# Steps of the mixers beneath the GEMMs, emitted with a priority 24 instructions later

## The chip, the cores and the metric

The kernel runs on one core of one Trainium2 chip, as one program. The metric is the device time of a launch in microseconds; the median of several runs is compared. A profiled execution gives the trace that is read here. Its engines are PE (TensorE), DVE (VectorE), ACT (ScalarE), POOL (GpSimd) and SP (SyncE, which issues most DMAs).

## The reference

One inference step of a decoder trunk with two layers and D = 1024, for a prompt of 1024 tokens and for 8 samples of 8 new tokens each, in float32. Cut to what matters:

```
for layer in range(2):
    h = rmsnorm(x, norm_pre_mix[layer])
    if layer == 0: # half of the heads GLA (linear attention with gates), half a 31-tap causal conv
        z = h @ w_in_even
        oa = rmsnorm(gla_scan(q, k, v, log_a, state)) * silu(r)
        c = silu(layernorm(causal_dwconv(ga * sigmoid(gg), conv_buf)))
        y = concatenate([oa, c]) @ w_out_even
    else:          # three groups of dilated attention with a T5 bias, and a chunked gMLP
        z = h @ w_in_odd
        oc = softmax-weighted sum of dilated_attn(q, kv, window, dilation, bias) over 3 groups
        od = gelu(du) * (tril(sgu_w) @ layernorm(gelu(dv)) + sgu_b)
        y = concatenate([oc, od]) @ w_out_odd
    x = x + rmsnorm(y, norm_post_mix[layer])
    h = rmsnorm(x, norm_pre_ffn[layer])
    up = causal_dwconv(h @ w_up, ffn_buf)      # 3 taps, 2 * 2816 channels
    g, val = split(up)
    x = x + rmsnorm((gelu(g) * val) @ w_down, norm_post_ffn[layer])
```

The outputs are y of both groups and the new states and K/V buffers.

## The kernel before

**Two halves.** The tokens are two halves. A holds 512 tokens of the prompt and is one piece of 512 columns; B holds the other 512 and the 64 sample tokens, as two pieces of 288 columns. Activations lie as [channels, tokens]. While PE does the large products of one half, the small work of the other half (its mixer, its norms) is done beneath them.

**GEMM products.** `gemm` multiplies a chunk of weights, [up to 1024, 128], with the activations in three passes, so that products of rounded parts give float32 exactness: high part of the weight by the activation's `hi` and by its `lo`, low part of the weight by `hi`. The PSUM tiles of a GEMM are named `g`, those of all other work `m`; so `g<-hi,whi`, `g<-lo,whi` and `g<-hi,wlo` are GEMM products and `m<-...` are products or transposes of mixers and norms, both mostly at line 227 (`mm`) and 224 (`tr`). A chunk is loaded by a DMA of SP into `raw`; `whi` is rounded from it on POOL (line 206) or ACT, and `wlo` = raw - whi is made by DVE or POOL (line 371). `fill` issues these three under `high_priority(self.ahead)`, ahead = 400 from the second projection on.

**ConvFFN.** `ffn_up` does a pair of GEMMs, copies the result to `u`, does the three taps on ACT and DVE (the tiles `c`, line 200), and makes `c * c` on DVE (line 197) and of it `hi` on ACT (line 209) and `lo` on DVE. `ffn` goes through six parts of 4 or 3 such pairs; the pairs of a part stand between the down products of the part before, which need them.

**Background.** `during` installs a generator `self.bg`, whose steps emit a few instructions each and then yield their weight; after each k of a GEMM `gemm` calls `pump`, which takes as many steps as the pace asks for; `drain` takes what is left at once.

```
    def pump(self, units):
        if self.bg is None:
            return
        self.acc += units * self.rate
        while self.acc > 0:
            w = next(self.bg, None)
```

What stands beneath what, with the times of the profiled execution before:

- up to about 380 us: the projection of layer 0, `in_even`, of A with the load of B's x, then with A's conv and GLA, then of B; `out_proj` of A, and the rest of `in_even` of B with A's norms.
- 412 to 870: the first FFN, of A in layer 0, above `mix0`: B's conv (tiles `cv`, 240 rows on DVE at line 200), B's GLA (`gla`, line 959 copies queries into `w`; `gla_sample` multiplies `w` and `km`), copies of cache rows and the FFN's state (`fst`).
- 870 to 935: the end of that FFN, the norms between it and layer 1 (`ss` holds sums of squares, which a product with `ones` adds up; line 427 is `sq_add`'s on POOL), and B's `out_proj`.
- then `in_odd` of A, with B's norms; 1100 to 1440 lies in the FFN of B in layer 0, above `mix1(A)` (A's attention and gMLP).
- 1740 to 1850: `in_odd` of B, above B's `gmlp` and `sample_scores`. gMLP's normalised values use a tile with the tag `kt`; PE multiplies it with the weights `sg`.
- then the FFN of A in layer 1 above `mix1(B)`, and last, with 2420 to 2756 in it, the FFN of B.

**What sets the order.** The program is scheduled ahead of time. Each instruction has a priority, its place in the order in which the code emits it; for each engine the scheduler goes through a simulated time line of its own and puts next, among the instructions whose inputs it thinks ready, the one with the earliest priority. On the chip each engine then works through its list strictly in that order. `tc.high_priority(n)` moves what is emitted within it n places forward.

Of the kernel before, what the change touches and what calls it, by code (L numbers as in the profile page):

```python
# [15 lines left out]
PSUM = bass.MemoryType.PSUM  # L16
# [33 lines left out]
def t5_bucket(dist):  # L50
    """Bucket of a distance, from the shapes alone."""
    max_exact = N_BUCKETS // 2
    dist = np.asarray(dist)
    d32 = np.maximum(dist, 1).astype(np.float32)
    ratio = np.log(d32 / np.float32(max_exact)).astype(np.float32) / np.float32(math.log(MAX_DIST / max_exact))
    large = max_exact + (ratio * np.float32(N_BUCKETS - max_exact)).astype(np.int32)
    large = np.minimum(large, N_BUCKETS - 1)
    return np.where(dist < max_exact, dist, large)


def shape_constants():
    """Masks, selections and one-hot tables that depend on the shapes only."""
# [4 lines left out]
    m = []  # L67
# [9 lines left out]
    # query order inside a dilation class: partition (j, i) of class r is position 16 i + 4 j + r  # L77
# [13 lines left out]
    # rows (batch, part, head, query) of a pair of dilation classes -> columns (batch, head, query) of a class and head pair  # L91
# [5 lines left out]
    # columns (batch, head, query) -> (batch, class pair, head, class, query)  # L97
# [12 lines left out]
    # new keys of a sample batch: rows (head, query), columns new keys; steps 0 and 1 of dilation 4, step 0 of 16  # L110
# [10 lines left out]
# projections of the second half before and after the out projection of the first  # L121
VB1, VB2 = ("u", "glr", "q", "k", "v0"), ("v1", "r")
# paces of the work that runs between products, cache tiles loaded ahead
VQ, LQ, SA, QS, QM, VW, SV = 12, 6, 4, 14, 90, 0.4, 3
# (half, layer): down product of the last part but one before which the last pair of up projections runs
# [13 lines left out]
class Kern:  # L139
    def __init__(self, ctx, tc, I, O):  # L140
# [19 lines left out]
        # of 16 weight chunks: rounded on ACT instead of Pool, remainder on Pool instead of DVE  # L160
        self.nw, self.hi_act, self.lo_pool = 0, 0, 0

# [11 lines left out]
    def wk(self, i, shape, dt=F32):  # L174
        """Working tile of at most 2 KB per partition, slot i."""
# [38 lines left out]
    def copy(self, out, in_):  # L214
        """Copies that either engine can take, in turn unless DVE is loaded."""
# [13 lines left out]
    def rstd(self, out, in_, scale):  # L229
        """out = (in * scale + eps) ** -0.5 for a few columns."""  # L230
# [5 lines left out]
    def during(self, gen, weight, products, wait=0):  # L236
        """Spread gen, whose steps yield their weights, over that many products of [1024, 128] with 512 columns,
        from the one after the first wait."""
# [3 lines left out]
    def pump(self, units):  # L242
# [3 lines left out]
        while self.acc > 0:  # L246
            w = next(self.bg, None)
# [12 lines left out]
    def merge(*gens):  # L260
        """Steps of several (generator, weight), each at the pace of its weight."""
# [20 lines left out]
    def vec_consts(self):  # L282
        nc, I, cp = self.nc, self.I, self.cp
        # per-channel vectors: rows of 128 channels, turned into columns
# [19 lines left out]
    def mix_consts(self):  # L304
# [14 lines left out]
        # conv taps of the Conformer module: [channel, tile, tap]  # L319
# [7 lines left out]
        # twice, for the high and the low part of its input  # L327
# [3 lines left out]
        # ConvFFN taps: [channel, (w0 | w1 | w2 | b), tile]  # L331
# [42 lines left out]
    def gemm(self, h, hs, w, k0, c0, m):  # L374
        """PSUM tiles (one per piece) of w[k0.., c0:c0+m]^T @ h."""
# [11 lines left out]
    def gemm_narrow(self, h, hs, w, c0, m):  # L387
        """Like gemm for few columns, in two passes: rows m.. of the result are the low part of the weights."""
# [13 lines left out]
    def split(self, h, src, tag_pool=None):  # L402
        """Exact two-part form of an activation tile."""
# [11 lines left out]
    def sq_add(self, h, ss, src, k):  # L415
        """Add the squares of a tile to the partial sums ss; when it is urgent, DVE sums every other tile."""
# [12 lines left out]
    def rms(self, h, src):  # L429
        """Reciprocal rms of each token from the sums of squares in the columns of src."""  # L430
# [6 lines left out]
    def rb(self, h, ss, r=None):  # L437
        """[128, n] tile whose rows all hold the reciprocal rms of each token."""
# [23 lines left out]
    def pre_norm(self, h, xt, ss, name, l, r=None):  # L462
        """RMSNorm of the tiles in xt (consumed); returns the split operand tiles."""
# [73 lines left out]
    def finish(self, h, y, ss, xs):  # L537
        """Last residual norm and the output rows, in steps; 14 in all."""
# [33 lines left out]
    def ffn_state(self, l):  # L572
        """Sample rows of the ConvFFN buffer as [channel, tile, (batch, row)]."""
# [12 lines left out]
    def ffn_up(self, h, hs, l, j):  # L586
        """One pair of up-projected tiles through conv, gelu and product; returns the split activation."""
# [36 lines left out]
    def x_rows(self, h, tmp, xs, out):  # L624
        """Token-major rows of a residual kept as channel tiles, as [block][half of the channels]; tiles in the arena of tmp."""
# [18 lines left out]
    def last_down(self, h, tmp, acts, l, part, y, xt):  # L644
        """Last down products, residual norm and output rows of the samples' half, for one range of tokens after the other:
        the norm of a range runs under the products of the next."""
# [9 lines left out]
        def rows(blocks, c1, sq):  # L656
            """r times the weighted sums, plus the residual."""
# [1341 lines left out]
```

## Time and profile before

| | |
|---|---|
| three runs | 2784.78, 2800.16, 2804.39 us (median 2800.16) |
| the profiled execution, from first to last instruction | 2798.1 us |
| PE busy | 2673.0 us, 96% |
| PE weight loads | 2366.4 us, 85% |
| DVE busy | 1757.6 us, 63% |
| ACT busy | 973.7 us, 35% |
| POOL busy | 1035.2 us, 37% |
| mean granted TensorE clock | 0.967 |
| moved by DMA | 355.83 MB, mean 127 GB/s |

The profiled execution has no time of its own beside its span; the span is what stands for it here. A busy PE is one on which a product is under way; the clock is the share of full speed that was granted to it. In rows of the trace the first number is the start in us, the second the duration, then come engine, line, operation, what it writes and from what (partitions x elements), how many; in brackets stands how long the engine had been idle before and what released it.

### The profile page before, as it was taken

To read this page: it belongs to the slowest core of one execution; us is meant where nothing else is said; L and a number is where in the kernel's file an instruction comes from. 1 tells how busy PE (TensorE), PEld (TensorE's weight loads), DVE (VectorE), ACT (ScalarE), POOL (GpSimd) and SP (SyncE) were. 2 spreads that over 40 slices of the span, in tenths; PEclk is the share of its full clock that TensorE was granted. 3 is DMA by queue.
4 is the path that set the end of the run, shared out by engine and by line. 5 is a ranking of instruction groups with operands and counts; after the bars stand their busy time and mean duration, and the time that the engine had idled before them with its cause. 6 is when DMAs were issued, how large, how long until landed. Compare 5 with 4: busy or idle time off the path is not lost.

```text
span 2798.1 us, 44057 instructions
## 1 busy us (share of the span) xinstructions
PE 2673.0 (96%) x16517; PEld 2366.4 (85%) x16517; DVE 1757.6 (63%) x3057; ACT 973.7 (35%) x2036; POOL 1035.2 (37%) x1159
## 2 busy tenths in 40 slices
PE   7989999999999999999999999889999898999999
PEld 6779887787888879999999979878877687999998
DVE  4888359899577655555547783556654348655555
ACT  4343445433453222324223241123332343322223
POOL 2322333432326434332437543552112165433333
PEclk9999989999999999999999999999989898999999
DMA  6433354445444554232224436884444143422232
GB/s 211 120 102 90 88 184 151 146 159 163 156 139 125 182 165 139 76 94 68 85 68 134 126 107 191 238 233 130 135 127 122 37 144 106 129 78 79 85 91 83
DMA packets 505005, 355.83 MB, mean 127 GB/s; under 512 B 29547, under 2 KB 461282, under 8 KB 504015
## 3 DMA queue, kind: packets, MB, share of 16 engines
q1 hardware_dynamic: 504791, 353.01, 41.6%
q8 instruction: 131, 2.15, 0.3%
q14 instruction: 83, 0.68, 0.1%
HBM read 306.43 MB, written 75.97 MB: 137 GB/s over the span
## 4 chain that ended last, share of the span: by engine, by line
PE 64%; DVE 10%; DMA 5%; POOL 4%; issue 3%; ACT 2%; SPq 1%; POOLq 0%; DVEq 0%; ACTq 0%
PE g L227 55%; PE m L227 7%; DVE cv L200 3%; PE m L224 2%; DMA kc<-qr 1%; DVE wlo L371 1%; DVE c L200 1%; POOL whi L206 1%; SPq L188 1%; DVE y L197 1%; DVE y L200 1%; POOL w L1677 1%; DVE lo L197 1%; POOL ss L427 1%; DMA raw<-in_w_up 1%
## 5 line engine op out<-in xcount | busy, mean ns | idle before, releaser
L227 PE MATMUL g<-hi,whi 128*128 128x288 f32 (+2 forms) x4440 | 1279.3, 336 | 32.2 <-ACT hi L209 9.7
L227 PE MATMUL g<-lo,whi 128*128 128x288 f32 (+2 forms) x4440 | 1268.1, 334 | 5.1 <-DVE lo L197 5.0
L227 PE MATMUL g<-hi,wlo 128*128 128x288 f32 (+1 forms) x4416 | 1260.9, 334 | 2.8 <-DVE wlo L371 2.6
L227 PEld LDWEIGHTS g<-hi,whi 128*128 128x128 f32 (+1 forms) x4440 | 777.5, 192 | 107.5 <-issue 25.5
L227 PEld LDWEIGHTS g<-lo,whi 128*128 128x128 f32 (+1 forms) x4440 | 776.8, 191 | 71.2 <-DVE lo L197 7.2
L227 PEld LDWEIGHTS g<-hi,wlo 128*128 128x128 f32 x4416 | 773.5, 192 | 70.5 <-issue 7.8
L371 DVE TENSOR_TENSOR wlo<-raw,whi 128x1024 fp32r<-128x1024 f32 (+2 forms) x382 | 404.5, 1059 | 443.4 <-POOL whi L206 347.6
L206 POOL TENSOR_SCALAR whi<-raw 128x1024 fp32r<-128x1024 f32 (+2 forms) x307 | 318.4, 1037 | 762.8 <-PE g L227 659.3
L371 POOL TENSOR_TENSOR wlo<-raw,whi 128x1024 fp32r<-128x1024 f32 (+2 forms) x94 | 193.0, 2055 | 418.1 <-ACT whi L209 349.7
L200 DVE SCALAR_TENSOR_TENSOR c<-u,dw,c 128x512 f32<-128x512 f32 (+3 forms) x528 | 316.6, 637 | 43.7 <-ACT c L212 42.2
L209 ACT ACTIVATE whi<-raw 128x1024 fp32r<-128x1024 f32 (+3 forms) x171 | 145.0, 848 | 361.7 <-PE g L227 219.3
L209 ACT ACTIVATE u<-g 128x224 f32<-128x224 f32 (+2 forms) x352 | 129.1, 398 | 249.7 <-PE g L227 236.9
L200 DVE SCALAR_TENSOR_TENSOR cv<-u,cvw,cv 128x512 f32<-128x512 f32 (+21 forms) x240 | 202.2, 853 | 4.0 <-ACT cv L212 2.1
L197 DVE TENSOR_TENSOR y<-y,g 128x288 f32<-128x288 f32 (+3 forms) x240 | 120.4, 525 | 117.4 <-PE g L227 117.0
L212 ACT ACTIVATE c<-g,dw 128x288 f32<-128x288 f32 (+1 forms) x264 | 173.1, 657 | 2.3 <-DMA out_s_ffn_conv<-rw 1.3
L209 ACT ACTIVATE hi<-c 128x512 fp32r<-128x512 f32 (+1 forms) x88 | 57.9, 658 | 222.6 <-DVE c L197 222.5
L427 POOL TENSOR_TENSOR ss<-ss,sq 128x512 f32<-128x512 f32 (+1 forms) x75 | 119.9, 1599 | 41.1 <-ACT sq L212 40.6
L212 ACT ACTIVATE c<-c 128x512 f32<-128x512 f32 (+1 forms) x88 | 57.9, 658 | 138.4 <-DVE c L200 131.9
L212 ACT ACTIVATE sq<-y 128x512 f32<-128x512 f32 (+3 forms) x103 | 63.3, 622 | 85.5 <-POOL ss L427 41.9
L200 DVE SCALAR_TENSOR_TENSOR y<-y,vec,rb 128x512 f32<-128x512 f32 (+1 forms) x104 | 87.5, 908 | 7.2 <-ACT rb L209 7.2
L1677 POOL TENSOR_TENSOR w<-kc,kc 128x512 f32<-128x512 f32 x48 | 65.1, 1368 | 69.4 <-DMA kc<-qr 57.8
L600 POOL COPY last<-u 128x2 f32<-128x2 f32 x88 | 45.8, 521 | 121.6 <-ACT u L209 102.3
(288 smaller groups left out, 2350.6 us busy)
## 6 DMA issues: line engine op xcount, KB each, us to landing
raw<-in_w_up SPq DMA_DIRECT2D x176, 512.0 KB
raw<-in_w_down SPq DMA_DIRECT2D x128, 256.0 KB
raw<-in_w_in_odd SPq DMA_DIRECT2D x44, 512.0 KB
raw<-in_w_in_even SPq DMA_DIRECT2D x40, 512.0 KB
out_s_kv<-in_cache_c_w SPq DMA_DIRECT2D x32, 512.0 KB
raw<-in_w_down SPq DMA_DIRECT2D x64, 192.0 KB
xl<-x SPq DMA_DIRECT2D x40, 256.0 KB
kc<-in_cache_c_w SPq DMA_DIRECT2D x80, 128.0 KB
```

The costliest lines, as they stand in the source:

```text
L188: self.nc.sync.dma_start(out, in_)
L197: self.nc.vector.tensor_tensor(out=out, in0=a, in1=b, op=op)
L200: self.nc.vector.scalar_tensor_tensor(out=out, in0=a, scalar=s, in1=b, op0=op0, op1=op1)
L206: self.nc.gpsimd.tensor_scalar(out=out, in0=a, scalar1=s1, scalar2=s2, op0=op0, op1=op1)
L209: self.nc.scalar.activation(out, in_, AF.Copy, scale=scale)
L212: self.nc.scalar.activation(out, in_, func, **kw)
L224: self.nc.tensor.transpose(out, in_, self.ident[:k, :k])
L227: self.nc.tensor.matmul(out, l, r, start=start, stop=stop)
L371: eng.tensor_tensor(out=wlo[:, :nk, :m], in0=raw[:, :nk, :m], in1=whi[:, :nk, :m].bitcast(F32), op=ALU.subtract)
L427: eng.tensor_tensor(out=t, in0=t, in1=sq, op=ALU.add)
L600: self.nc.gpsimd.tensor_copy(self.last2[l][:, jt, :], u[:, 512:514])
L1677: nc.gpsimd.tensor_tensor(out=pr, in0=kc.rearrange("p i c -> p (i c)"), in1=q.rearrange("p i c -> p (i c)"), op=ALU.mult)
```

## The change

`pump` takes its steps with a priority 24 places later. `high_priority(-24)` adds 24 to the place of each instruction that a step emits, DMAs included, so that it competes with GEMM instructions (products, weight fills, evictions, conv taps) that are emitted up to 24 instructions behind it. Fills within keep their own 400 places. `drain` takes its steps as before, and so does code that runs norms in a plain loop. Nothing else changes but comments, which shifts lines by 2 or 3 (197 is 199 after the change, 200 is 202, 209 is 211, 224 is 226, 227 is 229).

```diff
         self.ahead = 0
+        self.lag = 24
...
         while self.acc > 0:
-            w = next(self.bg, None)
+            with self.tc.high_priority(-self.lag):
+                w = next(self.bg, None)
             if w is None:
```

Every engine has the same instructions as before; what differs is their order. Three places, each first as it is before and then as it is now.

The first is on DVE in the first FFN (near 640 us of the trace). `c_1133` and `c_1143` are tiles of the FFN's conv, `cv_1110` and `cv_1228` those of B's conv in `mix0`, and line 197's row is the product `c * c` of which `hi` is made.

```order
L200 SCALAR_TENSOR_TENSOR c_1133_5623<-u_1134_5624,dw0_828,c_1133_5623 128x510
L200 SCALAR_TENSOR_TENSOR cv_1110_5441<-us_811_3799,cvw_823,cv_1110_5441 128x64
L200 SCALAR_TENSOR_TENSOR c_1143_5696<-u_1144_5697,dw0_828,c_1143_5696 128x511
L200 SCALAR_TENSOR_TENSOR cv_1228_6213<-u_530_2276,cvw_823,cv_1228_6213 128x512
L200 SCALAR_TENSOR_TENSOR cv_1228_6213<-us_812_3800,cvw_823,cv_1228_6213 128x64
L200 SCALAR_TENSOR_TENSOR cv_1110_5441<-u_494_2033,cvw_823,cv_1110_5441 128x512
L197 TENSOR_TENSOR c_1127_5584<-c_1127_5584,c_1133_5623 128x512
L200 SCALAR_TENSOR_TENSOR cv_1110_5441<-us_811_3799,cvw_823,cv_1110_5441 128x64
L200 SCALAR_TENSOR_TENSOR c_1143_5696<-u_1144_5697,dw0_828,c_1143_5696 128x510
```

```order
L202 SCALAR_TENSOR_TENSOR cv_1228_6213<-u_530_2276,cvw_823,cv_1228_6213 128x512
L202 SCALAR_TENSOR_TENSOR c_1143_5696<-u_1144_5697,dw0_828,c_1143_5696 128x511
L202 SCALAR_TENSOR_TENSOR c_1133_5623<-u_1134_5624,dw0_828,c_1133_5623 128x510
L202 SCALAR_TENSOR_TENSOR cv_1228_6213<-us_812_3800,cvw_823,cv_1228_6213 128x64
L202 SCALAR_TENSOR_TENSOR cv_1110_5441<-u_494_2033,cvw_823,cv_1110_5441 128x512
L202 SCALAR_TENSOR_TENSOR cv_1110_5441<-us_811_3799,cvw_823,cv_1110_5441 128x64
L202 SCALAR_TENSOR_TENSOR cv_1228_6213<-u_530_2276,cvw_823,cv_1228_6213 128x512
L202 SCALAR_TENSOR_TENSOR c_1143_5696<-u_1144_5697,dw0_828,c_1143_5696 128x510
L199 TENSOR_TENSOR c_1127_5584<-c_1127_5584,c_1133_5623 128x512
L202 SCALAR_TENSOR_TENSOR cv_1228_6213<-us_812_3800,cvw_823,cv_1228_6213 128x64
L202 SCALAR_TENSOR_TENSOR cv_1110_5441<-u_494_2033,cvw_823,cv_1110_5441 128x512
```

The product stands at DVE's place 832 before and 824 now: rows of `cv`, emitted earlier and given the later priority, now stand behind it.

The second is on PE at the end of the first FFN (870 us). `g_1531`, `g_1536` and `g_1541` are the last down products of A; `m_1479` and `m_1481` belong to `gla_sample`, `m_1496` and `m_1502` to the FFN's state.

```order
L227 MATMUL g_1531_7780<-hi_1403_7195,wlo_1530_7776 128x512
L227 MATMUL m_1479_7546<-w5_1442_7377,km_1478_7544 64x128 x8
L227 MATMUL m_1481_7560<-w5_1442_7377,km_1480_7558 64x128 x8
L224 MATMUL m_1496_7638<-ident_87,w3_1491_7605 128x64 x4
L224 MATMUL m_1502_7663<-ident_87,w1_1501_7661 128x16 x4
L227 MATMUL g_1531_7780<-hi_1452_7419,whi_1529_7775 128x512
L227 MATMUL g_1531_7780<-lo_1453_7420,whi_1529_7775 128x512
L227 MATMUL g_1531_7780<-hi_1452_7419,wlo_1530_7776 128x512
L227 MATMUL g_1536_7800<-hi_1369_7026,whi_1534_7795 128x512
```

```order
L229 MATMUL g_1541_7820<-hi_1452_7419,wlo_1540_7816 128x512
L229 MATMUL m_1464_7469<-ident_87,zt_1473_7506 64x128
L229 MATMUL m_1465_7470<-ident_87,zt_1473_7506 64x128
L229 MATMUL m_1464_7469<-w5_1442_7377,AT_935_4410 64x128
L229 MATMUL m_1464_7469<-ident_87,zt_1473_7506 64x128
L229 MATMUL m_1465_7470<-w5_1442_7377,AT_936_4412 64x128
L229 MATMUL m_1465_7470<-ident_87,zt_1473_7506 64x128
L229 MATMUL m_1475_7518<-w5_1442_7377,km_1474_7516 64x128 x8
L229 MATMUL m_1477_7532<-w5_1442_7377,km_1476_7530 64x128 x8
L229 MATMUL m_1479_7546<-w5_1442_7377,km_1478_7544 64x128 x8
L229 MATMUL m_1481_7560<-w5_1442_7377,km_1480_7558 64x128 x8
L226 MATMUL m_1496_7638<-ident_87,w3_1491_7605 128x64 x4
```

Before, these mixer rows stand between the down products, with `g_1531`, `g_1536` and `g_1541` still to come; now all of them, and the product of `ones` with `ss_1507` too, stand behind the last of `g_1541` and ahead of `g_1610`, the first product of B's `out_proj`.

The third is on PE in `in_odd` of B (1740 us and on). `m_3174` is a product of gMLP with the tile `kt`; `g_3164` and `g_3165` are the two pieces of one GEMM, `g_3190` and `g_3191` those of the next.

```order
L227 MATMUL g_3164_17258<-hi_2934_16034,whi_3162_17253 128x288
L227 MATMUL g_3165_17259<-hi_2934_16034,whi_3162_17253 128x288
L227 MATMUL g_3164_17258<-lo_2935_16035,whi_3162_17253 128x288
L227 MATMUL m_3174_17317<-sg_3067_16843,kt_3148_17201 64x128 x4
L227 MATMUL g_3165_17259<-lo_2935_16035,whi_3162_17253 128x288
L227 MATMUL g_3164_17258<-hi_2934_16034,wlo_3163_17254 128x288
L227 MATMUL g_3165_17259<-hi_2934_16034,wlo_3163_17254 128x288
L227 MATMUL g_3164_17258<-hi_2936_16051,whi_3162_17253 128x288
```

```order
L229 MATMUL g_3164_17258<-hi_2936_16051,wlo_3163_17254 128x288
L229 MATMUL g_3165_17259<-hi_2936_16051,wlo_3163_17254 128x288
L229 MATMUL g_3190_17371<-hi_2902_15893,whi_3188_17366 128x288
L229 MATMUL g_3191_17372<-hi_2902_15893,whi_3188_17366 128x288
L229 MATMUL g_3190_17371<-lo_2903_15894,whi_3188_17366 128x288
L229 MATMUL g_3191_17372<-lo_2903_15894,whi_3188_17366 128x288
L229 MATMUL g_3190_17371<-hi_2902_15893,wlo_3189_17367 128x288
L229 MATMUL g_3191_17372<-hi_2902_15893,wlo_3189_17367 128x288
L229 MATMUL m_3174_17317<-sg_3067_16843,kt_3148_17201 64x128 x4
L229 MATMUL g_3190_17371<-hi_2904_15910,whi_3188_17366 128x288
```

`m_3174` stood within the first GEMM; now the rest of that GEMM and six products of the next stand ahead of it.

## The prediction

> **What bounds the kernel now.** I read the page first, from its busy shares to its slices and its chain of waits.
>
> ```profile
> span 2798.1 us, 44057 instructions
> PE 2673.0 (96%) x16517; PEld 2366.4 (85%) x16517; DVE 1757.6 (63%) x3057; ACT 973.7 (35%) x2036; POOL 1035.2 (37%) x1159
> PE 64%; DVE 10%; DMA 5%; POOL 4%; issue 3%; ACT 2%; SPq 1%; POOLq 0%; DVEq 0%; ACTq 0%
> ```
>
> TensorE is busy in 2673.0 of 2798.1 us, so an order of instructions alone can win at most the 125.1 us in which it stands idle, and what its clock loses after such stops. The chain agrees: 64% PE. What matters is thus where PE stops, and whether the order changes there. I cut the run into its stages, and asked for PE's waits in the three where the new order moves mixer products against GEMM products and PE stops at all.
>
> ```profile
> core 0: us, PE busy (x) PEld busy (x) DVE busy (x) ACT busy (x) POOL busy (x), PEclk, DMA share, GB/s
> 412.00:560.00 148.00, 138.11 (x639) 111.55 (x639) 135.04 (x242) 73.07 (x115) 54.71 (x36) 0.94 0.45 146
> 560.00:660.00 100.00, 93.93 (x519) 75.57 (x518) 99.81 (x185) 38.58 (x64) 28.67 (x23) 0.97 0.44 142
> ...
> 870.00:935.00 65.00, 58.44 (x385) 55.15 (x384) 47.36 (x55) 21.16 (x42) 35.19 (x20) 0.92 0.42 135
> 1100.00:1440.00 340.00, 339.88 (x2384) 313.25 (x2383) 185.10 (x424) 111.69 (x294) 116.03 (x213) 1.00 0.29 84
> 1740.00:1850.00 110.00, 100.11 (x731) 96.87 (x731) 58.82 (x95) 21.46 (x54) 57.11 (x48) 0.95 0.86 245
> 2420.00:2756.00 336.00, 336.00 (x2525) 335.99 (x2525) 178.05 (x308) 92.03 (x230) 119.93 (x209) 1.00 0.28 82
> ...
> PE m L227 <- POOL w L959: 6.8, 1, 6.8
> PE g L227 <- ACT hi L209: 6.0, 2, 5.1
> PE g L227 <- DVE lo L197: 2.4, 2, 2.0
> PE m L227 <- DVE k L197: 0.7, 1, 0.7
> ...
> PE m L227 <- POOL ss L427: 3.4, 1, 3.4
> PE m L227 <- DVE ss L427: 1.6, 1, 1.6
> PE g L227 <- DVE lo L197: 1.6, 1, 1.6
> ...
> PE m L227 <- DVE kt L197: 8.3, 4, 3.2
> ```
>
> From 1100 to 1440 and from 2420 to 2756 us PE idles 0.12 and 0.00 us: there, with mix1(A) or no mixer, nothing can be won, although mix1(A)'s products move by about 20 GEMM products. The first FFN (412 to 870) loses 15.9 us in four kinds of wait, its end (870 to 935) 6.6, the layer-1 projection of the samples' half (1740 to 1850) 8.3 to the mixer's kt tile. That is 30.8 us of idle PE, all of it at places that move. DVE is full in the first FFN: 99.81 of 100 us between 560 and 660. Waits elsewhere, as those at the other handovers, stand at the same place in both orders, and I count them as unchanged.
>
> **The change part by part.** Nothing is added or removed; every number below is a move. Two prices first.
>
> ```profile
> 535.82 0.39 PE L227 MATMUL g<-hi,whi 128*128 128x512 f32 x1
> 542.39 0.39 PE L227 MATMUL g<-hi,wlo 128*128 128x512 f32 x1
> ...
> 1768.71 0.43 PE L227 MATMUL g<-hi,whi 128*128 128x288 f32 x2
> 1768.97 0.42 PE L227 MATMUL g<-lo,whi 128*128 128x288 f32 x2
> ```
>
> The first two rows are the first and the last of 30 GEMM products of the first half, so one costs 6.57 / 29 = 0.227 us; two of the samples' half cost 0.26, one 0.13. Now the stops.
>
> ```profile
> 550.31 1.65 PE L227 MATMUL m<-w,k 128*128 128x128 f32 x6 [6.77 <-POOL w L959]
> 551.61 0.77 PE L227 MATMUL g<-hi,whi 128*128 128x512 f32 x1
> ...
> 554.32 0.53 PE L227 MATMUL g<-hi,whi 128*128 128x512 f32 x1
> ...
> 536.56 1.26 POOL L959 COPY w<-q 64x256 f32<-64x256 f32 x1 [2.83 <-DVE q L197]
> 538.76 11.50 POOL L959 COPY w<-q 64x256 f32<-64x256 f32 x1 [0.94 <-DVE q L197]
> 550.22 2.35 POOL L371 TENSOR_TENSOR wlo<-raw,whi 128x1024 fp32r<-128x1024 f32 x1
> 552.53 1.75 POOL L600 COPY last<-u 128x2 f32<-128x2 f32 x2
> ...
> 643.31 1.22 PE L227 MATMUL g<-hi,whi 128*128 128x512 f32 x2 [5.06 <-ACT hi L209]
> ...
> 638.87 0.74 DVE L200 SCALAR_TENSOR_TENSOR c<-u,dw,c 128x510 f32<-128x510 f32 x1
> 641.91 0.69 DVE L197 TENSOR_TENSOR c<-c,c 128x512 f32<-128x512 f32 x1
> ```
>
> *The stop at 643.31.* It waits for hi, which ACT makes from the c-by-c product at 641.91, which DVE reaches late because it works through the conv's cv rows without a pause. In the new order that product stands 8 DVE places earlier (the first place shown above). From 638.87 to 641.91 six rows take 3.0 us, half a microsecond each, so 8 places are 4 us. PE comes there about as late as before. I take -4.
>
> *The stop at 550.31.* PE waits for a copy that held POOL 11.50 us. In the new order this mixer product stands 24 GEMM products later, 24 x 0.227 = 5.4 us of cover, but on POOL the copy now stands behind the 2.35 us weight remainder and one of the two small copies (1.75 for two), so it may come 3.2 us later. 5.4 - 3.2 = 2.2; I take -2, between -6.8 (gone) and +3 (the remainder's own input late).
>
> The Trainium skill, "SBUF — State Buffer", section "SBUF: two separate sides", says that VectorE and GpSimd share one port pair as an exclusive lock, the loser standing still for the whole instruction. This speaks against the change here: DVE's work is the same, so the 11.50 us stay. By it this term cannot pass -2.2; the trace agrees in so far as the copy at 536.56, of the same shape, took 1.26 us.
>
> *The other waits of the first FFN* (0.9 + 2.4 + 0.7 us): PE's places don't change at the first two, DVE's GEMM rows come some five places earlier. I take -1.5, between 0 and -4.
>
> *The clock.* The rows from 551.61 to 554.32 are the seven products behind that stop: six steps in 2.71 us, 0.45 each instead of 0.227, so 1.35 us lost. After a stop that shrinks under 2 us I count this as won: -1.5 for the stop at 643.31, none for 550.31.
>
> The Trainium skill, "TensorE: Matmul & The Clock Gate", Part 1, has the clock halve after an idle window of about 3.4 us and return after as much work. By that rule up to 1.7 us hang on each longer stop, and nothing on shorter ones; the spacing of 0.45 after the stop of 6.77 us agrees, and the sum would not differ by more than 1 us.
>
> *The end of the first FFN.*
>
> ```profile
> 851.26 1.96 PE L227 MATMUL m<-w,km 64*64 64x128 f32 x32
> ...
> 902.46 0.38 PE L227 MATMUL m<-ones,ss 128*128 128x1 f32 x2 [3.36 <-POOL ss L427]
> 905.35 3.15 PE L227 MATMUL m<-ones,ss 128*128 128x1 f32 x14 [1.63 <-DVE ss L427]
> ```
>
> Before, the mixer's last products (m<-w,km and some transposes) stand between the last FFN products; 32 of them, the first row here, cost 1.96 us. Now they stand behind them (second place above), so the last y comes 2 to 4 us earlier, and with it the two norms that lead to in_odd(A). What PE has left to do grows by as much. PE's 6.6 us of waiting are what this can give. But PE now meets the product of the ones with ss 90 GEMM products earlier (90 x 0.13 = 12 us), and waits there unless ss comes as much earlier; what it skips, it does afterwards. I take half, -3.5, between -7.5 (with a microsecond of clock) and +3.
>
> *The projection at 1740 to 1850.* The four stops on kt total 8.3 us; their products stand 15, 13, 6 and 18 GEMM products later (third place above shows the first). 52 x 0.13 = 6.8 us of cover; DVE's kt comes a place or two later. I take -4.5, between -8.3 and 0.
>
> *In in_even(B)*, two more:
>
> ```profile
> 161.67 3.41 PE L227 MATMUL m<-glr,wg 32*128 32x512 f32 x4 [2.29 <-DMA glr<-zglr]
> 175.58 2.06 PE L227 MATMUL m<-q,k 64*128 64x128 f32 x32
> 180.23 0.40 PE L227 MATMUL g<-hi,whi 128*128 128x288 f32 x1 [2.60 <-ACT th L212]
> ```
>
> The first gets 12 products of cover, 12 x 0.13 = 1.6 us won. At the second, 12 of the 16 mixer products ahead now stand behind: 1.5 of the 2.06 us no longer fill the time in which PE waits for a PSUM bank anyway, 1.5 us lost. Together 0.
>
> *The queues at the start.* The second weight load moves from place 37 to 19 of SP's queue, past the loads of x for the second half, and its remainder on DVE from place 37 to 11. The first weight was issued at 11.02; the next at 23.58:
>
> ```profile
> 14.85 1.06 POOL L206 TENSOR_SCALAR whi<-raw 128x1024 fp32r<-128x1024 f32 x1 [1.88 <-DMA raw<-in_w_in_even]
> 29.41 3.99 POOL L206 TENSOR_SCALAR whi<-raw 128x1024 fp32r<-128x1024 f32 x2 [13.49 <-DMA raw<-in_w_in_even]
> ```
>
> So a load takes 3.8 to 5.8 us; DVE, in order, may stand a microsecond behind it. +0.5, between -1 and +3. Later in the run SP's moves are small (two places on average), since weight loads already ran ahead by priority 400.
>
> *New waits.* What was put later is needed somewhere: each drain, each FIFO on DVE, ACT and POOL whose head now is a GEMM row not yet ready. The trace can't show these; the 8 stops above are what the old order left, 31 us in all. I take +4, bounds 0 and +25.
>
> Sum: -4 - 2 - 1.5 - 1.5 - 3.5 - 4.5 + 0 + 0.5 + 4 = -12.5 us. From the span of 2798.1 this is 2785.6; the median of the three runs lies 2.1 above the span (2800.16, from 2784.78 to 2804.39), which gives **2787.7, said as 2788**.
>
> **The rivals.**
>
> *It only slides* (about 2799). A mixer product is put in when the planner thinks its input is ready; delayed producers delay their consumers, and the stops travel along. For it: DVE's mixer rows move later too, by three places, 1.5 us. Against: on PE they move 21 to 30 products, 5 to 7 us, in the first FFN.
>
> *All stops go* (about 2758). 30.8 us idle, plus the slow clock behind them: 1.35 us at 550, about as much at 643, 5 at 902 (PEclk 0.92 over 65 us) and 2 at 1740, some 10. For it: DVE gives GEMM rows precedence just where it is full. Against: the 11.50 us copy, and PE's earlier arrival at ss.
>
> *Slower: POOL's blocked instruction hits a weight* (about 2822). Somewhere in the first FFN POOL stands still while DVE runs without a pause, as at 538.76. If, in the new order, the victim is a weight remainder instead of a mixer's copy, GEMM products wait for it: a down product of 12 rows gives 12 x 0.227 = 2.7 us of cover, two of them 5.4, so a block of 11.5 costs 6.1 us and 1.4 of clock. It decides from a remainder of over 5.4 us, and POOL does half of them there; three such blocks are 22.5 us, with the gains at 550 to 643 (7.5 of them) lost and the other half kept: about 2800 + 22. The one remainder shown above took 2.35 us, which speaks against it.
>
> The skill's lock rule named above is this rival's mechanism; the trace bears it out by one copy of 11.50 us.
>
> **How the numbers follow.** Forecast 0.42, slides 0.24, all stops go 0.20, slower 0.14. The forecast's own range is 2770 to 2806 from its bounds. The 8-in-10 range reaches to most of both outer rivals: 2755 to 2812; under it about half of "all stops go", over it most of "slower". A change under 1% (28 us) can't be told from none here, the three runs alone spreading 0.7%. Faster by over 1%, below 2772: 0.17 of "all stops go" and 0.07 of the forecast, 0.24. Slower by over 1%, above 2828: 0.07 of "slower" and 0.02 of unknown waits, 0.09. Within 1%: 0.67.
>
> **What would show it.** The stop on hi near 643 falls under 1.5 us, the one on POOL's w to 3 to 6; the waits for kt in the projection total under 4.5 us; PE's idle time at 870 to 935 falls under 4. PE's busy time stays within 10 us of 2673. If POOL's L371 rows take far more than the 2.35 us shown, or PE waits on wlo, the slower rival is at work; if the waits keep their names and sizes at shifted times, it only slid. I am wrong if the planner's view of DVE's load is so far off that new waits of more than 25 us appear in stages that I counted as still.

## The result, and the profile after

Five runs of the changed kernel have a median of 2818.2 us (2816.01 to 2825.93), against 2800.16 us before (2784.78 to 2810.03). The ratio is 1.0077, with a 95% interval from 1.0051 to 1.0102: the change made the kernel slower by 0.8%. The forecast was 2788 us, in a range from 2755 to 2812. The profiled execution spans 2814.0 us, 15.9 more than before.

The page of the changed kernel, its span and busy times:

```profile
span 2814.0 us, 44031 instructions
PE 2701.7 (96%) x16517; PEld 2368.8 (84%) x16517; DVE 1758.3 (62%) x3057; ACT 971.0 (35%) x2034; POOL 1006.8 (36%) x1159
```

PE does the same 16517 products and is busy 28.7 us longer (2701.7 against 2673.0). (Not every engine has quite the same instructions, as was said of the change: ACT_TABLE_LOAD stands 28 times on ACT instead of 30, and semaphore instructions are 24 fewer; these are the 26 by which the first line differs.) So it is not waits that made the kernel slower: idle time fell, from 125.1 to 112.3 us. To see where, I cut both traces at the same GEMM products (the first product of the first FFN, the same product in `in_odd` of A, and so on), first before, then after:

```profile
0.00:414.11 414.11, 375.47 (x2223) 326.67 (x2223) 264.99 (x447) 163.12 (x324) 116.60 (x83) 0.94 0.43 133
414.11:1022.14 608.03, 581.11 (x3000) 478.98 (x3000) 485.47 (x808) 245.82 (x439) 233.34 (x172) 0.97 0.48 152
1022.14:1440.07 417.93, 417.81 (x2848) 383.69 (x2847) 217.45 (x469) 129.65 (x335) 142.70 (x248) 1.00 0.32 94
1440.07:2000.10 560.03, 529.19 (x3250) 480.14 (x3249) 353.35 (x540) 172.00 (x343) 254.20 (x249) 0.98 0.54 159
2000.10:2420.06 419.96, 398.30 (x2412) 326.74 (x2411) 235.45 (x440) 156.86 (x333) 151.99 (x174) 0.91 0.38 115
```

```profile
0.00:397.74 397.74, 365.47 (x2222) 316.67 (x2222) 265.50 (x447) 159.96 (x321) 114.88 (x83) 0.98 0.45 138
397.74:1022.93 625.19, 608.38 (x2999) 486.29 (x3000) 487.09 (x807) 247.50 (x440) 212.74 (x172) 0.97 0.47 148
1022.93:1449.37 426.44, 424.03 (x2849) 382.90 (x2848) 217.77 (x469) 131.73 (x337) 136.77 (x248) 1.00 0.31 92
1449.37:2009.80 560.43, 530.39 (x3250) 480.92 (x3249) 353.08 (x540) 171.95 (x343) 253.22 (x249) 0.97 0.53 159
2009.80:2436.00 426.20, 402.25 (x2412) 331.92 (x2412) 233.42 (x441) 153.87 (x331) 152.69 (x174) 0.90 0.37 113
```

The second number of a row is the stage's length, the third PE's busy time. The stages differ by -16.4, +17.2, +8.5, +0.4 and +6.2 us; the rest, 378.0 us, is equal. In the first FFN and its end (second row) PE waits 10.1 us less and yet is busy 27.3 us longer, at the same clock of 0.97. This is the row that decides.

What PE does there is seen in the timeline. Before, 32 of the mixer's small products, between two GEMM products:

```profile
624.10 0.26 PE L227 MATMUL m<-q,k 64*32 64x32 f32 x8
625.09 0.39 PE L227 MATMUL m<-q,k 64*32 64x32 f32 x24 [0.73 <-DVE k L197]
625.41 0.50 PE L227 MATMUL g<-hi,whi 128*128 128x512 f32 x1
```

After, the same products, and PE's weight loads (PEld) at that place:

```profile
611.43 0.39 PE L229 MATMUL g<-hi,wlo 128*128 128x512 f32 x1
611.66 0.39 PE L229 MATMUL g<-hi,whi 128*128 128x512 f32 x1
611.98 0.24 PE L229 MATMUL m<-q,k 64*32 64x32 f32 x2
612.15 0.50 PE L229 MATMUL g<-lo,whi 128*128 128x512 f32 x1
612.58 0.25 PE L229 MATMUL m<-q,k 64*32 64x32 f32 x2
612.76 0.49 PE L229 MATMUL g<-hi,wlo 128*128 128x512 f32 x1
...
611.43 0.19 PEld L229 LDWEIGHTS g<-hi,whi 128*128 128x128 f32 x1
611.97 0.13 PEld L229 LDWEIGHTS m<-q,k 64*32 64x32 f32 x2 [0.35 <-DVE c L202]
612.15 0.19 PEld L229 LDWEIGHTS g<-lo,whi 128*128 128x128 f32 x1
612.58 0.14 PEld L229 LDWEIGHTS m<-q,k 64*32 64x32 f32 x2 [0.24 <-issue]
612.75 0.19 PEld L229 LDWEIGHTS g<-hi,wlo 128*128 128x128 f32 x1
```

In the columns behind the operation stand the weights (rows*columns) and the moving operand. The block of 24 took 0.32 us. Now two mixer products alternate with one GEMM product, and one such round takes 0.61 us (612.15 to 612.76), where a GEMM product alone takes 0.23 (611.43 to 611.66). Nothing is shown as idle, but the weight loads tell: between two GEMM products the load of the next weights begins while the product before is under way (611.43, for the product at 611.66); the other four begin together with their own product, and PEld stands still 0.24 us before the mixer's at 612.58, for "issue", that is for nothing that the profile names. Between the two kinds PE's weights are no longer loaded ahead.

How it comes about is in the priorities. A `high_priority` context gives the places used in it back at its end. So a step's rows and the GEMM rows emitted after it carry the same numbers, 24 apart or not, and the scheduler deals them out in turn; `lag_zero` below, with 0 places, bears this out. In the orders, runs of mixer rows between GEMM rows on PE went from 419 to 608, in the first FFN from 78 to 202; changes from full weights (128*128) to partial ones (fewer rows or columns) went from 257 to 346, in the first FFN from 49 to 113, in the FFN of B from 66 to 84.

### The profile page after: what moved, and what is told of

It reads as the page before. It is cut to its first block, busy times and chain, and to the rows that moved or that the text cites. A ratio compares the mean times of both kernels' runs of the same rounds, so it can differ in the third digit from the quotient of the medians.

```text
span 2814.0 us, 44031 instructions
## 1 busy us (share of the span) xinstructions
PE 2701.7 (96%) x16517; PEld 2368.8 (84%) x16517; DVE 1758.3 (62%) x3057; ACT 971.0 (35%) x2034; POOL 1006.8 (36%) x1159
## 4 chain that ended last, share of the span: by engine, by line
PE 60%; DVE 10%; DMA 5%; POOL 3%; issue 3%; SPq 1%; ACT 1%; DVEq 0%; POOLq 0%; ACTq 0%
PE g L229 52%; PE m L229 7%; DVE cv L202 3%; PE m L226 2%; DVE wlo L374 2%; DVE c L202 1%; POOL whi L208 1%; DMA kc<-qr 1%; DVE y L199 1%; SPq L190 1%; DMA raw<-in_w_up 1%; DMA raw<-in_w_down 1%; DVE lo L199 1%; POOL S L208 1%; DVE y L202 0%
## 5 line engine op out<-in xcount | busy, mean ns | idle before, releaser
L229 PE MATMUL g<-hi,whi 128*128 128x288 f32 (+2 forms) x4440 | 1280.0, 336 | 26.4 <-ACT c L214 7.0
L208 POOL TENSOR_SCALAR whi<-raw 128x1024 fp32r<-128x1024 f32 (+2 forms) x307 | 309.1, 1007 | 768.0 <-PE g L229 676.0
L374 POOL TENSOR_TENSOR wlo<-raw,whi 128x1024 fp32r<-128x1024 f32 (+2 forms) x94 | 185.0, 1970 | 414.1 <-ACT whi L211 319.2
```

Source lines behind the costliest of these rows:

```text
L208: self.nc.gpsimd.tensor_scalar(out=out, in0=a, scalar1=s1, scalar2=s2, op0=op0, op1=op1)
L229: self.nc.tensor.matmul(out, l, r, start=start, stop=stop)
L374: eng.tensor_tensor(out=wlo[:, :nk, :m], in0=raw[:, :nk, :m], in1=whi[:, :nk, :m].bitcast(F32), op=ALU.subtract)
```

## The experiments

**Where it is lost, and whether it is the 24 places.** In the first three runs the change is active in one part of the program only; `lag` None means that `pump` is as before.

```diff
-            with self.tc.high_priority(-self.lag):
-                w = next(self.bg, None)
+            if self.lag is None:
+                w = next(self.bg, None)
+            else:
+                with self.tc.high_priority(-self.lag):
+                    w = next(self.bg, None)
...
+        self.lag = None     # start_only: 24 up to here; ffn1_only: None up to here, 24 from here
         self.during(mix0(), 210, 61)
...
+        self.lag = 24       # rest_only, None up to here; ffn1_only: None from here on
         for _ in norms(A, y, ss, 1, "norm_post_ffn", 0, "norm_pre_mix", 1, hA):
```

In the fourth, `self.lag = 0` stands in place of 24, with the context as it is.

> Steps are emitted with the later priority only until the first FFN begins; from there on pump is as before (no priority context at all). PE's order has 425 runs of mixer rows between GEMM rows, against 419 before and 608 after the change. Theory 1 (what costs time is that PE changes more often between GEMM and mixer products, 0.22 us per extra run in the first FFN; the start gains for a reason of its own): the 16.7 us gained ahead of 412 us stay and nothing is lost, about 2783 us. Rival (work is only put off, and the start's gain is paid back in the first FFN): about 2800 us, with the first FFN longer by some 15 us.

> Later priority only for the steps beneath the first FFN (539 runs of mixer rows on PE, 198 of them in that FFN, against 78 there before). Theory 1: 120 extra runs at 0.22 us are 26 us more of busy PE in 412 to 1022 us, less about 10 us of waits that go: about 2816 us. Rival (the loss in the first FFN came from work put off at the start): about 2790 us, by the waits that go.

> Later priority only from the end of the first FFN on (481 runs on PE, 62 more than before). Theory 1: 44 extra runs beneath the FFN of B cost 6 to 8 us at 0.14 to 0.18, the other 18 some 3, and the longer waits for gMLP's tile about 5: about 2814 us. Rival (nothing but waits counts; those of the projection of B shrink): 2795 us or less.

> The steps stand in the priority context as in the changed kernel, but with an offset of 0 in place of 24. The context gives back its places at its end, so the GEMM rows behind a step get the same numbers as the step's own rows. PE's order has 609 runs of mixer rows, as the changed kernel (608). Theory 1: as slow as the changed kernel in the first FFN, 20 to 28 us more busy PE there, 2810 to 2825 us in all. Rival (the 24 places are what costs): as before, 2800 us, for nothing is put off.

| kernel | median, us | ratio to before (95%) | first FFN and end: length, PE busy | partial changes there |
|---|---|---|---|---|
| start_only | 2784.72 | 0.9972 (0.9952 to 0.9992) | 610.5, 584.2 | 49 |
| ffn1_only | 2812.59 | 1.0070 (1.0043 to 1.0097) | 627.5, 609.5 | 113 |
| rest_only | 2804.51 | 1.0041 (1.0020 to 1.0062) | 605.5, 582.8 | 49 |
| lag_zero | 2824.61 | 1.0131 (1.0088 to 1.0175) | 627.0, 614.9 | 122 |

The times came 2 us over the 2783 said (`start_only`), 3 under the 2816 (`ffn1_only`), 9 under the 2814 (`rest_only`) and within the range (`lag_zero`). The parts add up: -0.28, +0.70 and +0.41% are +0.83%, and the whole is +0.77%. The loss in the first FFN is made there, and is no payment for the start. And it does not need the 24 places: with 0, nothing is put off, the context alone deals the rows out, and the kernel is about as slow (one of its four runs, 2846.78 us, lifts its ratio; the others took 2820.36 to 2825.63). The one rival that `rest_only` could have borne out (fewer waits, less time) fell too.

**What a change between the two kinds costs.** `switch_bench` and `switch_bench_2` leave the whole step out; in each, products on constants alternate or stand in runs.

```diff
+        for kind in kinds:
+            for per in (1, 2, 4):
+                for _ in range(16):
+                    g()                      # 128x512, rounded type
+                    for _ in range(per):
+                        m(kind)
+            ...                              # 16 g, then 32 m(kind), then 32 g
```

> Leaves out the whole step: PE does only products on constants. GEMM products (128x512, rounded type) alternate with 1, 2 or 4 small products, or both stand in runs of their own; the small ones are of six kinds: three shapes and a transpose in plain float32 (m<-xf,yf or m<-ident,yf) and two shapes in the rounded type of the GEMM (m<-xr,yr). Theory 1 (each change from GEMM to mixer products and back costs PE some 0.2 us): a pattern of one GEMM product and two small ones takes about 0.2 us more than the same three rows in runs of their own, for the shapes of the mixers in float32; whether the rounded type pays it too tells whether the type or the shape is what costs. Rival (the products last longer in the first FFN because other engines load the memory): alternating and grouped rows cost the same here, where nothing else runs.

> Leaves out the whole step, as the first run of products alone; the small products are float32 in other shapes: weights of 64x32 columns of result from both halves of the rows in turn, 64x128, 128x64, 64x64, the last two in turn, and 128x128. Theory 2: each pattern with partial weights pays 0.33 us each time that it goes to them and back, whichever side is cut; 128x128 pays nothing; two kinds of partial weights in turn pay each time too. Rival (only weights with few rows, not those with few columns, cost): 128x64 pays nothing.

Three pieces of the first one's timeline: small products with 64*64 weights in turn with GEMM products, the same in runs, and products with 128*128 weights in turn.

```profile
302.57 0.27 PE L227 MATMUL m<-yr,xr 64*64 64x128 f32 x1
302.77 0.50 PE L227 MATMUL g<-hi,whi 128*128 128x512 f32 x1
303.20 0.27 PE L227 MATMUL m<-yr,xr 64*64 64x128 f32 x1
...
336.37 3.92 PE L227 MATMUL g<-hi,whi 128*128 128x512 f32 x16
340.22 2.12 PE L227 MATMUL m<-yr,xr 64*64 64x128 f32 x32
342.27 2.99 PE L227 MATMUL g<-hi,whi 128*128 128x512 f32 x12
...
264.36 0.22 PE L227 MATMUL m<-yr,xr 128*128 128x128 f32 x1
264.42 0.45 PE L227 MATMUL g<-hi,whi 128*128 128x512 f32 x1
264.70 0.22 PE L227 MATMUL m<-yr,xr 128*128 128x128 f32 x1
```

In turn, a pair with partial weights takes 0.63 us (302.57 to 303.20). In runs, the GEMM product takes 0.24 (3.85 / 16) and the small one 0.064 (2.05 / 32), together 0.30: 0.33 us for each trip there and back, with no other engine at work. With full weights a pair takes 0.34, and in runs 0.23 + 0.11 = 0.34: nothing is lost. Worked out likewise for the other patterns:

| small product's weights | in turn, one each | the two in runs | a trip costs |
|---|---|---|---|
| 64*64, rounded type | 0.63 | 0.30 | 0.33 |
| 64*64, float32 | 0.78 | 0.45 | 0.33 |
| 64*128, float32 | 0.84 | 0.46 | 0.38 |
| 128*64, float32 | 0.78 | 0.45 | 0.33 |
| 128*128, float32 | 0.45 | 0.45 | 0 |
| 128*128, rounded type | 0.34 | 0.34 | 0 |
| transpose, 128*128 | 0.34 | 0.34 | 0 |

So it is neither the type nor the mixer as such; it is whether the weights fill the array, and 64 rows or 64 columns cost it alike. 64*64 and 128*64 in turn among themselves cost 0.14 us a row more than each alone (0.36 against 0.22). The first patterns of both runs (64*64 weights with 32 columns of result) fell for the most part into half clock and are not used.

The Trainium skill, "TensorEngine Tiling (Array Packing)", section "Key Properties", has the rule, which the prediction did not use: changing the tiling mode, not just the tile, drains TensorE. These runs agree, if partial weights count as a mode of their own, which no run shows by itself; they add the price, 0.33 to 0.38 us there and back.

**The theory sharpened, on the kernel itself.** If only partial weights cost, it must matter which mixer rows are kept together, not how many runs there are. All PE rows of a step (`lag24_grouped`), those with partial weights, or those with full ones, get one common place:

```diff
+            self.step, self.base = True, self.tc.cur_priority + self.lag
             with self.tc.high_priority(-self.lag):
                 w = next(self.bg, None)
+            self.step = False
...
     def mm(self, out, l, r, start, stop):
+        places = self.tc.cur_priority
+        if self.step:    # part_together: and min(l.shape[0], l.shape[-1]) < P; full_together: not so
+            self.tc.cur_priority = self.base
         self.nc.tensor.matmul(out, l, r, start=start, stop=stop)
+        if self.step:    # likewise
+            self.tc.cur_priority = places
```

`tr` is changed in the same way.

> As the changed kernel, but all PE rows of one step get one and the same place, 24 behind the step's start, so that they stay together; 472 runs of mixer rows on PE instead of 608, 102 instead of 202 in the first FFN. Theory 1: busy PE in 412 to 1022 us falls from 608 to about 586 us, the gain of the start stays: 2790 to 2800 us in all. Rival (the order on the other engines is what costs): as the changed kernel, 2815 us or more.

> As the changed kernel, but those PE rows of a step whose weights fill only part of the array (fewer than 128 rows or columns) get one common place, 24 behind the step's start; the others are as in the changed kernel. PE's order then changes 273 times from full to partial weights (257 before, 346 after the change), while its runs of mixer rows are still 527 (419 and 608). Theory 2 (only the change between full and partial weights costs, 0.33 us there and back): 73 x 0.33 = 24 us less busy PE than the changed kernel, 2790 to 2798 us. Theory 1 as first put (any change between GEMM and mixer rows costs 0.15 us): 81 x 0.15 = 12 us less than the changed kernel, 2803 to 2807 us.

> The other way round: the PE rows of a step with full 128x128 weights get the common place, those with partial weights are as in the changed kernel. 538 runs of mixer rows, but 346 changes from full to partial weights, as many as in the changed kernel. Theory 2: as the changed kernel, 2812 to 2820 us. Theory 1 as first put: 70 x 0.15 = 10 us less, 2805 us, the same as the run before it.

| kernel | runs of mixer rows | partial changes | median, us | ratio (95%) |
|---|---|---|---|---|
| changed kernel | 608 | 346 | 2818.2 | 1.0077 (1.0051 to 1.0102) |
| lag24_grouped | 472 | 289 | 2809.14 | 1.0038 (1.0021 to 1.0054) |
| lag24_part_together | 527 | 273 | 2804.60 | 1.0021 (1.0008 to 1.0034) |
| lag24_full_together | 538 | 346 | 2830.98 | 1.0115 (1.0093 to 1.0136) |

The last two have nearly as many runs (527 and 538) and lie 26.4 us apart; 73 partial changes at 0.33 us are 24. Theory 1 had them at the same time, so it falls. Taken singly the times don't show this: `lag24_part_together` lies within theory 1's range (2803 to 2807), and against theory 2 all three are late. `lag24_grouped` came 9 us later than its range (PE is busy 591.9 us in the first FFN's stage, where 586 was said), `lag24_part_together` 7 us and `lag24_full_together` 11 us. The rows of the last two for the first FFN's stage:

```profile
402.00:1021.00 619.00, 594.07 (x2999) 486.80 (x2999) 484.49 (x807) 246.36 (x440) 219.01 (x172) 0.96 0.48 149
403.73:1039.00 635.27, 616.03 (x3000) 493.19 (x3000) 486.72 (x807) 247.77 (x439) 223.04 (x172) 0.96 0.46 145
```

The first row is the kernel with partial rows together: 594.07 us busy, 13 over before, of which its 12 extra changes explain 4; and it idles 24.9 us, nearly as before (26.9), so it lost the waits that the change had saved. The second is busy 8 us longer than the changed kernel with the same count. What is left of both differences lies in the granted clock, which is 0.96 in these two rows and 0.97 in those of before and after. At a slower clock the same products last longer: behind the stop at 550.31, where the trace has a clock of 0.5, a GEMM product takes 0.45 us instead of 0.227. Busy time multiplied by the granted clock of the stage (here with more digits than the rows show) estimates what its products take at full clock:

| kernel | partial changes there | PE busy, us | granted clock | product, us |
|---|---|---|---|---|
| before, start_only, rest_only, x_load_only | 49 | 581.0 to 584.2 | 0.9656 to 0.9715 | 564.1 to 564.5 |
| lag24_part_together | 61 | 594.1 | 0.9579 | 569.1 |
| lag24_grouped | 66 | 591.9 | 0.9738 | 576.4 |
| changed kernel | 113 | 608.3 | 0.9746 | 592.9 |
| ffn1_only | 113 | 609.4 | 0.9701 | 591.2 |
| lag24_full_together | 113 | 616.0 | 0.9596 | 591.2 |
| lag_zero | 122 | 614.9 | 0.9642 | 592.9 |

Equal counts now give equal times to 2 us. Each further change costs 0.38 to 0.44 us, somewhat more than in the products alone; only `lag24_grouped` pays more, 0.70, and has 10 more changes among kinds of partial weights, which explain a part of it. With this theory 2 holds in the kernel too. Why the clock was lower in `lag24_part_together` and `lag24_full_together` is not shown.

**Later PE rows alone.** Here every product is wrapped in a context of its own; rows of a step get 24 or 96 places more, the step's other rows none.

```diff
+        self.lag = 0
+        self.lag_pe, self.step = 24, False    # or 96
...
-        self.nc.tensor.matmul(out, l, r, start=start, stop=stop)
+        with self.tc.high_priority(self.lag - self.lag_pe if self.step else 0):
+            self.nc.tensor.matmul(out, l, r, start=start, stop=stop)
```

> Only the PE rows of a step get the later place (24, each for itself); all other rows of a step keep theirs, and the step gives its places back. 379 runs on PE, 40 less than before, 78 in the first FFN. Theory 1: busy PE in the first FFN as before (581 us), 40 fewer runs save 6 to 8 us elsewhere: about 2785 us unless new waits come. Rival (mixer products that come later make what hangs on them late): 2805 us or more, by waits.

> As the last one with 96 places in place of 24: 257 runs on PE, 162 fewer than before. Theory 1 alone: 162 x 0.15 to 0.22 us are 24 to 36 us less busy PE, 2765 to 2775 us. Rival: the mixers' products now come late, and waits of 10 to 40 us appear where a half's mixer has to be done; 2790 us or more.

They took 2931.74 us (ratio 1.0478, 1.0459 to 1.0496) and 3025.76 us (1.0812, 1.0788 to 1.0835): the rivals held, by far more than they said. With the wrapping GEMM products take no places either, so 24 places should reach over several GEMMs; this is argued from the code, not shown. PE idles 213.5 us in the first (125.1 before), at a granted clock of 0.942 (0.967 before). The longest waits of the first:

```profile
PE m L232 <- DVE kt L200: 28.5, 4, 9.5
PE m L228 <- DVE w L200: 22.3, 7, 7.3
PE m L228 <- DVE w L206: 19.6, 5, 7.1
PE m L232 <- POOL ss L435: 16.7, 2, 16.1
```

Behind the colon stand us in total, how often, and the longest. These four stood at 8.3, 5.5, 1.3 and 8.6 us before. With 379 and 257 runs these kernels have the fewest of all, and are the slowest: here mixers that come late cost far more than the changes between kinds. That price had no place in theory 1, whose numbers were wrong here. (Partial changes in their traces did not fall much, 270 and 240 against 268 before.)

**Where the start gains.** The lag ends where the first background, B's load of x, is drained:

```diff
         self.in_even(A, st[0]["hs"], st[0], ("u",))
+        self.lag = None
         self.ahead = 400
         self.drain()
```

> The later priority only for the first background, the load of B's x beneath the first projection of A (to about 85 us); all else as before. Theory A (the start gains because weight loads and what makes weights of them go ahead of the loads of x, on SP's queue and on the engines): most of the 8 us that the start gained is here, 2788 us. Theory B (the start gains beneath the rest of the projections, by the order of the conv and GLA steps): 2795 us, as before.

It took 2797.28 us, a ratio of 1.0005 (0.9986 to 1.0024): nothing of the gain is there, so theory A falls and theory B is left. PE's waits between 100 and 330 us, first of `x_load_only`, then of `start_only`:

```profile
PE m L229 <- DMA glr<-zglr: 6.9, 1, 6.9
PE m L229 <- DVE k L199: 4.5, 2, 4.2
PE g L229 <- ACT th L214: 2.9, 2, 2.7
```

```profile
PE m L229 <- DMA glr<-zglr: 3.1, 1, 3.1
PE g L229 <- ACT th L214: 2.2, 3, 1.4
PE m L229 <- DVE k L199: 0.4, 2, 0.3
```

Beneath the projections GLA's first steps make PE wait for `k`; with the later priority this wait falls to 0.4 us. Without it it was 4.5 us in three traces (`before`, `ffn1_only`, `x_load_only`), but 1.8 in `rest_only`, so 1.4 to 4.1 us are won. (The wait for `glr`, a load, was 2.3 us in the trace before, so its difference here says nothing.) The granted clock up to the first FFN was 0.98 after and in `start_only`, 0.94 to 0.96 in these four; that shorter waits made it so is not shown, and where the rest of the 8 us comes from stays open. `start_only` keeps the gain and has none of the losses: at 0.9972 it is the one version faster than the kernel before, by 8 us.

## Why the prediction was wrong, point by point

**The step that failed** is the sentence "Nothing is added or removed; every number below is a move", with products priced at their own length wherever they stand. It asked how far a mixer row moves, and never what it stands between afterwards. For consecutive GEMM products of the first FFN and its end, I took the time between their starts, less idle time and less a GEMM product's own 0.2275 us (0.1325 for 288 columns). The intervals with partial weights in them rose from 38 to 106, and their sum from 49.5 to 75.0 us, 0.375 us for each new one; those with full weights alone rose from 40 to 96 and cost 3.2 us more, with 29 more rows, which had stood among partial ones before; all others 1.4 us less. That is the 27.3 us of that stage. In the FFN of B, where "nothing can be won", 18 partial changes at 0.33 are 5.9 us of the 6.2 that PE is busy longer; that nothing can be lost there was never shown. Over the whole program 89 changes at 0.33 are 29 us, and PE is busy 28.7 us longer; that these agree so well is partly luck, since the first stage is 10.0 us less busy at a faster clock (0.98 against 0.94), and the other stages 38.7 us more. The count was there to be had in the orders; the third place shown even has mixer and GEMM rows side by side.

The rival "slower" (2822 us) came within 4 us of the median, by luck: its reason was POOL. It needed weight remainders of over 5.4 us and three blocks of 7.5 us; the longest POOL remainder in the first FFN took 3.93 us after the change, and PE waited 5.0 us there for remainders in all.

**The waits** fell, but not by the terms said. In the first FFN (396 to 871 us) they now are:

```profile
PE g L229 <- DVE wlo L374: 4.1, 5, 1.6
PE m L229 <- DVE S L199: 3.9, 1, 3.9
PE g L229 <- DVE lo L199: 1.3, 2, 1.0
PE g L229 <- POOL wlo L374: 0.9, 2, 0.6
PE g L229 <- ACT whi L211: 0.7, 1, 0.7
PE m L229 <- POOL w L962: 0.3, 1, 0.3
```

- *643.31*: the wait for hi is gone, 5.1 us won where -4 was said.
- *550.31*: -2 was said; the wait for POOL's w fell from 6.8 to 0.3, since the copy of 11.50 us did not recur. This hangs on the order, not on chance: `start_only`, `rest_only` and `x_load_only`, with the old order in this FFN, have the copy at 11.50 us again, `ffn1_only` has none over 1.23. DVE was as busy as before (485.47 and 487.09 us in that stage), so the conclusion drawn in the prediction from the Trainium skill, "SBUF — State Buffer", section "SBUF: two separate sides", that these 11.50 us stay with DVE's work, did not hold. The groups of these copies in the two traces, with their sum and mean in ns, first before:

```profile
L959 POOL COPY w<-q 64x256 f32<-64x256 f32 x20 | 24.6, 1243 | 34.0 <-PE m L227 18.4 <-DVE q L197 15.6
L962 POOL COPY w<-q 64x256 f32<-64x256 f32 x20 | 14.0, 709 | 39.2 <-DVE q L199 29.5 <-PE m L229 5.3 <-DVE wlo L374 4.3
```

- *New waits*: +4 was said; in the first FFN wlo, S and whi are new, 9.6 us. They are smaller than what went, 14.3 us, where 7.5 was said. So the net of -4.7 us is near the -3.5 said by luck: both terms were mis-sized, and the errors cancel.
- *The end of the first FFN*: -3.5 was said; the waits there fell from 6.6 to 4.1 us.
- *The projection of B*: -4.5 was said; the waits for kt rose from 8.3 to 13.6 us. The cover that I counted did not exist, since the chain that makes kt begins with PE rows that moved as well. Before, the transposes of dv stand 52 to 60 GEMM products ahead of their kt product; after, 52 to 63. The last of them after the change:

```profile
1831.97 0.27 PE L226 MATMUL m<-ident,dv 128*64 128x128 f32 x1
...
1846.15 0.69 PE L229 MATMUL m<-sg,kt 64*64 64x64 f32 x8 [6.46 <-DVE kt L199]
```

  The rival "it only slides" is nearer here, but the waits also grew. Five kernels whose steps are 24 places later in this stage wait 11.4 to 15.0 us for kt, the five in which nothing is put off there 6.9 to 8.6. From the last transposes of dv to the last kt product it takes 14.2 us after and 9.2 before; on DVE two more reductions and one more weight remainder then stand among the rows of that chain.
- *The start*: 0 and +0.5 were said. The two profiled executions differ by -16.4 us there, but before's was itself late: `ffn1_only`, `rest_only` and `x_load_only`, which have no lag on the GLA and conv steps there, reach the first FFN at 408.6, 405.8 and 409.3 us. The runs show -8 us (`start_only`). The term was mis-sized.
- *2000 to 2420 us*: +6.2 in the trace. In `rest_only`, with the lag there as in the changed kernel, the stage takes 420.4 us, as before; this difference is not shown to be the change's. What `rest_only` loses in its trace is 11 us beneath the FFN of B (428.9 us there, 417.9 before).

PE's idle time fell by 12.8 us in all, and the forecast's sum was -12.5; that is luck too, since 6.4 of it lies ahead of the first FFN, where nothing was said to be won. PE's busy time was to stay within 10 us of 2673, and that is the line which told at once that the reason was not on the list.

## What to carry to other kernels

Before pricing a new order of instructions, count in it how often the bounding engine changes between kinds of work, above all between full and partial weights on TensorE; a trip cost 0.33 us here with products alone, one and a half GEMM products, and about 0.4 us in the kernel, and shows as busy time, not as a wait. A scheduler's priority that gives two streams the same numbers shuffles them row by row; keep rows with partial weights of one step together. That took back most of the loss here, but the kernel was still no faster than before (1.0021). A product moved later covers a wait only if what makes its input stays where it was.

## What the hardware showed that was not expected

- Alternating full 128*128 weights of a GEMM with full weights of other products costs nothing, in float32, in the rounded type and for transposes (0.34 and 0.45 us in turn as in runs), while weights cut to 64 rows, 64 columns or both cost 0.33 to 0.38 us there and back.
- With nothing but products on PE (the two benches), a load of partial weights behind a product with full ones began 0.07 us before the end that the profile gives that product (ends are modelled), all 392 times; a load between two products with full weights began at least 0.22 us before that end.
- One POOL copy of 64x256 took 11.50 us in the trace before and in the three with the old order in the first FFN; in the eight other traces of the whole kernel none took over 3.92 us (1.23 after the change, with DVE as busy). What blocks it was not settled.
